# GLA outputs transposed in 32x32 blocks on VectorE and placed by the DRAM round trip, with the head scale in the gating

## The chip, the cores and the metric

The kernel runs on one core of a Trainium2 chip. The metric is the device time of one execution in microseconds. Three runs of the kernel before gave 1454.77 us in the median (1454.15 to 1455.24). The profile is of one further execution, whose span from the first to the last instruction is 1455.4 us.

## The reference, cut to what matters

One inference layer is computed for a prompt of 1024 tokens and for 8 sample tokens. The normalised input is multiplied with one wide matrix; from the product three branches are made, each gated by a SiLU of its own columns, and merged:

```python
h = rmsnorm(x, norm_gain)
q, k, v, gla_g, a_lr, u, pool_g, xq, xg, merge = jnp.split(h @ w_in, split_pts, axis=-1)
o, S = gla_chunked(q, k, v, log_a, S0)                  # 4 heads, values of 256
o = rmsnorm(o, gla_gain.reshape(GLA_HEADS, GLA_DV))     # per head, with a gain per value column
br_gla = o * jax.nn.silu(gla_g)
p, new_hist = multiscale_pool(u, pool_hist, pos0, pool_w, pool_scale)   # windows 2/4/8/16, then a 256x256 map
br_pool = p * jax.nn.silu(pool_g)
br_x = cross_attn(xq, mem_k, mem_v) * jax.nn.silu(xg)
merged = sum over the branches of sigmoid(merge_n) * (br_n @ w_branch[n])
y = x + merged @ w_out
```

The change touches the path from `o` to `br_gla` for the prompt tokens: the recurrence gives `o` with tokens on the partitions, and the gating wants it with value columns on the partitions.

## The kernel before, in words

**The wide product.** `w_in` is taken in pairs of 128 columns (class `Pair`). A pair is done with seven products instead of eight (a Strassen-like scheme): `operands` (L291-315) makes seven left operands a11, a12, s2, s1, s3, s4, a22 from the loaded weights `raw`, on VectorE the sums `ws` (L302), and of each operand a high and a low part: the high part by a copy on ScalarE (L221, tiles `a11h`, `s4h`, ...) and the low part by a subtraction on VectorE (L222, tiles `a11l`, `s4l`, ...). Parts live in a ring of 8 buffers (`W2`, L127). `product` (L533) does one of the seven products: two halves `c` of 258 columns, 4 x 3 matmuls each (high by high L240, high by low L241, low by high L242). `run_product` (L541) puts the results together: a product's result in PSUM is saved by a ScalarE copy (L550, tiles `r1`, `r2`, `r3`), and VectorE adds products to it (L598 for the second product, L615 for the fifth, L624 for the sixth), which releases the PSUM banks `p.z` and `p.x`, of which six exist (`PX`, L96). The order of products (`seq`, L334) is 0 to 4 of a pair, then product 0 of the next pair, then 5 and 6.

**The gated pairs.** The last twelve pairs carry the gates: `gate` applies SiLU, `finish` (L562) multiplies with the branch's output `mix` (L571), then with the sample columns (L573), and sends the tile to DRAM. `mixed(e)` (L580) loads the branch's output tiles `mix` from `mix_scr` on SyncE (L649, in `loaded`) one product ahead of their use. The gated pairs are, in order, those of cross-attention (n = 2), of the GLA branch (n = 0), and of pooling (n = 1). The GLA ones stand at about 915 to 1007 us.

**What fills the products.** After each half product `emit` (L1231) puts steps of two other streams between the matmuls (`fill`, L1222): first cross-attention and the GLA recurrence (from about 390 to 760 us), then, while the GLA gates are computed, pooling. Pooling goes group by group (`w` = 2, 4, 8, 16) and chunk by chunk of 256 tokens: `windows(c)` makes the trailing sums `sw` by 1 to 4 doublings on VectorE (L1143), the mean minus token `df` (L1151; L1149 and L1150 for the first tokens), and its high and low part (`dfh` on ScalarE, `dfl` on VectorE); `mixed(c)` multiplies `dfh` and `dfl` with the group's map in 12 matmuls into a bank `pz` (L240-242 with `dfh`, `dfl`), of which two exist.

**The GLA outputs.** `gla_out(h, c)` (L964) is called 16 times, for 4 heads and 4 chunks. `on` holds 256 tokens by 256 values, as two blocks of 128 tokens. Four TensorE transposes (L971) bring it into a bank `pz`, two ScalarE copies with the head's gain as scale (L973) bring it to `go`, and a DMA from the GpSimd queue (L974) writes it to `mix_scr`.

**What sets the order.** TensorE and SyncE issue in the order in which the program is written (`manual_schedule`, L94). The instructions of VectorE, ScalarE and GpSimd are put into an order by the framework's scheduler when the kernel is built; the order is then fixed, and each engine goes through its list in order, waiting at an instruction until its inputs are there.

Of the kernel before, what the change touches and what calls it, by code (L numbers as in the profile page):

```python
# [14 lines left out]
AF = mybir.ActivationFunctionType  # L15
ALU = mybir.AluOpType
AX = mybir.AxisListType

P = 128
D = 1024  # L20
T = 1024
# [3 lines left out]
NH = 4  # L25
DK = 128
DV = 256
# [6 lines left out]
CT = 256  # L34
# [13 lines left out]
def trunk_kernel(ctx: ExitStack, tc: tile.TileContext,  # L48
# [3 lines left out]
    nc = tc.nc  # L52
# [21 lines left out]
    def act(out, x, func, **kw):  # L74
        i = nc.scalar.activation(out, x, func, **kw)
        if func in (AF.Sigmoid, AF.Silu):
            table["others"].append(i)
            for e in table["exps"]:
                tc.add_manual_dep(i.ins, e.ins.name, nosync, reason="table set")
        else:  # L80
            tc.add_manual_dep(i.ins, table["load"].ins.name, nosync, reason="table set")
            table["new"].append(i)
        return i
# [12 lines left out]
    def PX():  # L96
        return ps.tile([P, 512], F32, tag="px", name="px", bufs=6)

    def PZ():
        return ps.tile([P, 512], F32, tag="pz", name="pz", bufs=2)  # L100

    def shaped(t, shape):
        n = math.prod(shape)
        t = t[:, :n]
        if len(shape) == 2:
            t = t.rearrange("p (a b) -> p a b", a=shape[0])
        elif len(shape) == 3:
            t = t.rearrange("p (a b c) -> p a b c", a=shape[0], b=shape[1])
        return t

    def E(shape, dt=F32, name="e"):
        return shaped(ep.tile([P, EW], dt, tag="e", name=name), shape)

    def R(shape, dt=F32, name="r"):

        return shaped(wk.tile([P, 512], dt, tag="ring", name=name, bufs=NR), shape)
# [13 lines left out]
    def Q(name):  # L130
        return wk.tile([P, QT], F32, tag="q", name=name, bufs=5)
# [5 lines left out]
    ident = cp.tile([P, P], F32, name="ident")  # L137
# [27 lines left out]
    ngain, ggain, pscale, bav = vec[:, 0:8], vec[:, 8:16], vec[:, 16:24], vec[:, 24:28]  # L165
# [35 lines left out]
    def scratch(n, name, shape):  # L201
        return [dr.tile(list(shape), F32, name=f"{name}{i}") for i in range(n)]
# [5 lines left out]
    al_scr = scratch(2, "als", (P, HT))  # L208
    q_scr, k_scr, v_scr4 = (scratch(n, s, PAIR) for n, s in ((2, "qsc"), (2, "ksc"), (4, "vsc")))
    u_scr, xq_raw = (scratch(4, s, PAIR) for s in ("usc", "xqsc"))  # L210
    mix_scr = [scratch(4, f"mixsc{n}_", (P, 2, T)) for n in range(3)]
    m_scr = [scratch(4, f"msc{n}_", PAIR) for n in range(3)]
    br_scr = [scratch(4, f"brsc{n}_", PAIR) for n in range(3)]

# [318 lines left out]
    def product(acc, n, start):  # L533
        i, j = seq[n]
        lh, ll = left[i, j]
        for c in range(2):
            for k in range(4):
                hi, lo = ops[RIGHT[j]][k // 2]
                rh, rl = (x[:, k % 2, c * QT:(c + 1) * QT] for x in (hi, lo))
                mm3(acc[c][:, :QT], lh[:, k, :], ll[:, k, :], rh, rl, start and k == 0, k == 3, not start)  # L540
            yield c  # L541

    def run_product(n):

        i, j = seq[n]
        p = pairs[i]

        def saved(acc, c, name):
            r = Q(name)
            nc.scalar.activation(r, acc[c][:, :QT], AF.Copy)  # L550
            return r

        def piece(t, h, c):
            return t[:, h, c * QT:(c + 1) * QT]

        def diagonal(x, e):

            if e == 0:
                return x[:, 0:16].rearrange("p (a b) -> p a b", b=4)[:, 0:4:3]
            return x[:, 4:12].rearrange("p (a b) -> p a b", b=4)  # L560

        def finish(t, e):  # L562
            rows = (slice(0, 4, 3), slice(1, 3))[e]
            if p.s0 is not None:
                nc.gpsimd.tensor_copy(diagonal(smp[:, NS * p.s0:], e), t[:, :, 512:HT])
            if p.gated:
                n, g = p.gated
                for i in range(2):
                    ch, hf = divmod((0, 3, 1, 2)[2 * e + i], 2)
                    m = p.mix[e][i]  # L570
                    nc.vector.tensor_tensor(t[:, i, :512], t[:, i, :512], m, op=ALU.mult)  # L571
                ss = diagonal(brs[n].rearrange("p k b -> p (k b)")[:, 2 * NS * g:], e)
                nc.vector.tensor_tensor(t[:, :, 512:HT], t[:, :, 512:HT], ss, op=ALU.mult)  # L573
            nc.gpsimd.dma_start(out=p.dst[:, rows, :], in_=t)

        def gate(t, h):
            if p.gated:
                act(t[:, h], t[:, h], AF.Silu)

        def mixed(e):  # L580

            if p.gated:
                n, g = p.gated
                for i in range(2):
                    ch, hf = divmod((0, 3, 1, 2)[2 * e + i], 2)
                    p.mix[e].append(loaded(mix_scr[n][g][:, ch, 512 * hf:512 * hf + 512], [512], "mix"))

        if j == 0:
            p.x = [PX() for _ in range(2)]
            p.r1, p.mix = [], ([], [])  # L590
            for c in product(p.x, n, True):
                p.r1.append(saved(p.x, c, "r1"))
                yield
        elif j == 1:
            y = [PX() for _ in range(2)]
            p.e1 = E([2, HT], name="c1")
            for c in product(y, n, True):
                nc.vector.tensor_tensor(piece(p.e1, 0, c), y[c][:, :QT], p.r1[c], op=ALU.add)  # L598
                if c:
                    gate(p.e1, 0)  # L600
                yield
        elif j == 2:
            p.r2 = []
            for c in product(p.x, n, False):
                p.r2.append(saved(p.x, c, "r2"))
                yield
        elif j == 3:
            p.z = [PX() for _ in range(2)]
            mixed(0)
            for c in product(p.z, n, True):  # L610
                yield
        elif j == 4:
            for c in product(p.x, n, False):
                r3 = saved(p.x, c, "r3")
                nc.vector.tensor_tensor(piece(p.e1, 1, c), p.z[c][:, :QT], r3, op=ALU.add)  # L615
                if c:
                    gate(p.e1, 1)
                    finish(p.e1, 0)
                yield
        elif j == 5:  # L620
            p.e2 = E([2, HT], name="c2")
            mixed(1)
            for c in product(p.z, n, False):
                nc.vector.tensor_tensor(piece(p.e2, 0, c), p.z[c][:, :QT], p.r2[c], op=ALU.add)  # L624
                if c:
                    gate(p.e2, 0)
                yield
        else:
            for c in product(p.x, n, False):
                dst = piece(p.e2, 1, c)  # L630
                if p.gated:
                    act(dst, p.x[c][:, :QT], AF.Silu)
                else:
                    nc.scalar.activation(dst, p.x[c][:, :QT], AF.Copy)
                if c:
                    finish(p.e2, 1)
                yield
# [6 lines left out]
    def mix_chunk(n, h, c):  # L644
        return mix_scr[n][h][:, :, c * CT:(c + 1) * CT]

    def loaded(src, shape, name, alloc=None):
        t = (alloc or R)(shape, name=name)
        nc.sync.dma_start(out=t, in_=src)  # L649
        return t  # L650
# [313 lines left out]

    def gla_out(h, c):
        on, _ = gla["o", h, c]
        g = R([2, CT], name="go")
        t = PZ()
        for i in range(2):
            for j in range(2):  # L970
                nc.tensor.transpose(t[:, i * CT + j * P:i * CT + (j + 1) * P], on[:, j, i * P:(i + 1) * P], ident)  # L971
        for i in range(2):
            nc.scalar.activation(g[:, i], t[:, i * CT:(i + 1) * CT], AF.Copy, scale=ggain[:, 2 * h + i:2 * h + i + 1])  # L973
        nc.gpsimd.dma_start(out=mix_chunk(0, h, c), in_=g)  # L974

    def gla_rows(h):

# [308 lines left out]
    with tc.issue_after(last["hi"].ins), tc.issue_after(last["lo"].ins):  # L1286
        prepare(1)
        for j in (4, 6):
            r = squares(x_t[j:j + 2], 4 + j)
# [166 lines left out]
    for hf, order in enumerate(ORDERS):  # L1456
        for tb in order:
            m = P if tb < 8 else NS
# [22 lines left out]
            n, a = hf, 0  # L1481
            for b in ends:
                t = ts if tb == 8 else begun.pop(0) if begun else PX()
# [13 lines left out]
                n, a = n + 1, b  # L1497
# [3 lines left out]
            if end:  # L1501
                r = rstd_of(sq[:, 2:3], 1.0 / D, more=so_far)
# [6 lines left out]
            r = rstd_of(sq[:, 0:1], 1.0 / D, m)  # L1509
# [34 lines left out]
```

## Time and profile before

| what | before |
|---|---|
| median of 3 runs | 1454.77 us |
| span of the profiled execution | 1455.4 us |
| TensorE matmuls busy | 1430.4 us, 98 % |
| TensorE weight loads busy | 1369.2 us, 94 % |
| VectorE busy | 896.6 us, 62 % |
| ScalarE busy | 688.4 us, 47 % |
| GpSimd busy | 159.0 us, 11 % |
| mean granted TensorE clock | 0.998 |
| DMA traffic | 259.46 MB, 181843 packets |

The page names engines PE, PEld (weight loads of TensorE), DVE (VectorE), ACT (ScalarE), POOL (GpSimd) and SP (SyncE). A group's row reads: line, engine, operation, out<-in tile names, count, then durations. A row of the timeline gives the start and the duration in microseconds; an instruction's successor on the same engine can start before the duration is over, so steps are read as differences of starts. A "q" behind an engine's name is its sequencer, which issues DMAs and waits. The matmul ends are modelled, so that a busy TensorE is not one at its peak.

### The profile page before, as it was taken

What the parts mean: (1) busy time and instruction counts of PE and PEld (TensorE: products, weight loads), DVE (VectorE), ACT (ScalarE), POOL (GpSimd) and SP (SyncE); (2) the same over time, 40 slices, a digit from 0 to 9 for tenths busy, and PEclk for the clock granted to TensorE, in tenths of its full rate; (3) what the DMA queues carried; (4) which work ended last, traced back from release to release, by engine and by line L of the source; (5) the groups of instructions that cost most, each with busy time, mean ns of one, the idle gap of its engine ahead of it and who ended that gap; (6) DMA issues with size and microseconds to landing.
All of it is one profiled execution on the core that took longest, in us unless ns stands there. A gap on an engine that the chain in (4) does not pass through costs nothing.

```text
span 1455.4 us, 28240 instructions
## 1 busy us (share of the span) xinstructions
PE 1430.4 (98%) x10817; PEld 1369.2 (94%) x10817; DVE 896.6 (62%) x2075; ACT 688.4 (47%) x1591; POOL 159.0 (11%) x297
## 2 busy tenths in 40 slices
PE   7999999999999999999999999999999999999998
PEld 6899999999899999999999999999999999999876
DVE  6955756656576767766756668785672443544436
ACT  5744444444565666656554445454472333233312
POOL 3211111111011111111111111110010000000000
PEclk9999999999999999999999999999999999999999
DMA  9345675756445453553544455464595677632633
GB/s 322 127 165 183 204 226 173 227 174 201 158 146 178 149 176 121 166 175 118 180 139 141 153 187 187 147 197 155 191 304 159 219 252 249 231 120 67 230 119 116
DMA packets 181843, 259.46 MB, mean 178 GB/s; under 512 B 20540, under 2 KB 130900, under 8 KB 181700
## 3 DMA queue, kind: packets, MB, share of 16 engines
q1 hardware_dynamic: 159900, 183.87, 40.8%
q0 software_dynamic: 21664, 73.59, 13.3%
q8 instruction: 85, 1.39, 0.4%
q14 instruction: 50, 0.41, 0.1%
q10 hardware_dynamic: 144, 0.20, 0.0%
HBM read 180.47 MB, written 77.59 MB: 177 GB/s over the span
## 4 chain that ended last, share of the span: by engine, by line
PE 87%; DMA 6%; DVE 4%; ACT 1%; issue 1%; SPq 0%; DVEq 0%; POOL 0%; ACTq 0%
PE px L240 25%; PE px L241 24%; PE px L242 24%; PE pz L242 2%; PE pz L240 2%; PE pz L241 2%; DMA qb<-xqs 2%; DMA raw<-in_w_in_dram 1%; DMA vc<-in_cache_mem_v_dram 1%; DVE kc L756 1%; PE pz L942 1%; PE pz L924 1%; DMA wm<-in_w_mv_dram 1%; PE pz L796 1%; PE pz L926 1%
## 5 line engine op out<-in xcount | busy, mean ns | idle before, releaser
L242 PE MATMUL px<-bh,wbl 128*128 128x384 f32 (+1 forms) x576 | 184.1, 320 | 0.0
L241 PE MATMUL px<-bl,wbh 128*128 128x384 f32 (+1 forms) x576 | 184.1, 320 | 0.0
L240 PE MATMUL px<-bh,wbh 128*128 128x384 f32 (+1 forms) x576 | 183.8, 319 | 0.0
L550 ACT ACTIVATE r<-px 128x258 f32<-128x258 f32 x240 | 89.8, 376 | 46.7 <-PE px L242 46.1
L240 PEld LDWEIGHTS px<-bh,wbh 128*128 128x128 f32 x576 | 108.4, 188 | 0.0
L241 PEld LDWEIGHTS px<-bl,wbh 128*128 128x128 f32 x576 | 108.2, 188 | 0.0
L242 PEld LDWEIGHTS px<-bh,wbl 128*128 128x128 f32 x576 | 108.2, 188 | 0.0
L240 PE MATMUL px<-ot,s1h 128*128 128x258 f32 x320 | 93.9, 293 | 0.0
L240 PE MATMUL px<-ot,s3h 128*128 128x258 f32 x320 | 93.4, 292 | 0.0
L240 PE MATMUL px<-o,a12h 128*128 128x258 f32 x320 | 93.3, 291 | 0.0
L240 PE MATMUL px<-o,s4h 128*128 128x258 f32 x320 | 93.0, 291 | 0.2 <-DVE c L615 0.2
L240 PE MATMUL px<-o,a11h 128*128 128x258 f32 x320 | 92.9, 290 | 0.0
L240 PE MATMUL px<-ot,a22h 128*128 128x258 f32 x320 | 92.9, 290 | 0.0
L240 PE MATMUL px<-ot,s2h 128*128 128x258 f32 x320 | 92.3, 288 | 0.0
L241 PE MATMUL px<-o,a11h 128*128 128x258 f32 x320 | 91.0, 284 | 0.3 <-DVE o L222 0.3
L242 PE MATMUL px<-o,a12l 128*128 128x258 f32 x320 | 90.7, 283 | 0.0
L241 PE MATMUL px<-o,a12h 128*128 128x258 f32 x320 | 90.6, 283 | 0.0
L241 PE MATMUL px<-ot,s2h 128*128 128x258 f32 x320 | 90.1, 282 | 0.5 <-DVE ot L222 0.5
L242 PE MATMUL px<-o,a11l 128*128 128x258 f32 x320 | 90.6, 283 | 0.0
L241 PE MATMUL px<-ot,a22h 128*128 128x258 f32 x320 | 90.5, 283 | 0.0
L242 PE MATMUL px<-ot,s3l 128*128 128x258 f32 x320 | 90.4, 283 | 0.0
L241 PE MATMUL px<-ot,s3h 128*128 128x258 f32 x320 | 90.4, 282 | 0.0
(469 smaller groups left out, 4587.3 us busy)
## 6 DMA issues: line engine op xcount, KB each, us to landing
raw<-in_w_in_dram SPq DMA_DIRECT2D x80, 512.0 KB, 3.8
msc<-c POOLq DMA_DIRECT2D x24, 516.0 KB, 4.4
brsc<-c POOLq DMA_DIRECT2D x24, 516.0 KB, 4.0
sig<-msc SPq DMA_DIRECT2D x24, 516.0 KB, 6.0
mix<-mixsc SPq DMA_DIRECT2D x48, 256.0 KB, 4.5
brr<-brsc SPq DMA_DIRECT2D x48, 256.0 KB, 5.3
wbr<-in_w_branch_dram SPq DMA_DIRECT2D x24, 512.0 KB, 5.5
acc<-sig POOLq DMA_DIRECT2D x16, 516.0 KB, 6.1
```

Of the source, the lines that this page charges most:

```text
L240: nc.tensor.matmul(out, lhsT=lh, rhs=rh, start=start, stop=False, skip_group_check=more)
L241: nc.tensor.matmul(out, lhsT=lh, rhs=rl, start=False, stop=False, skip_group_check=more)
L242: nc.tensor.matmul(out, lhsT=ll, rhs=rh, start=False, stop=stop, skip_group_check=more)
L550: nc.scalar.activation(r, acc[c][:, :QT], AF.Copy)
L756: nc.vector.tensor_tensor_reduce(kc[:, a, :], kc[:, a, :], qb[:, bb, :], scale=1.0, scalar=0.0, op0=ALU.mult, op1=ALU.add, accum_out=sc[:, ...
L796: nc.tensor.matmul(t[32 * j:32 * j + 32, :DV], lhsT=pm[:, a, 4 * i + j, :], rhs=vc[j][:, a, :], start=a == 0, stop=a == 1)
L924: nc.tensor.matmul(t[0:64, 0:P], lhsT=ki[:, 0:64], rhs=qi, start=True, stop=True)
L926: nc.tensor.transpose(t[:, P:2 * P], kt, ident)
L942: nc.tensor.matmul(to, lhsT=kiqi[:, 1, cs], rhs=st, start=False, stop=True)
```

## The change

`gla_out` no longer uses TensorE or ScalarE. One VectorE instruction transposes `on` (128 x 512) inside each 32x32 block, and the tile goes to a new DRAM scratch `on_scr[h]`. That has a row of 1 KB for each block of 32 tokens and each value column modulo 32; in a row the eight blocks of columns follow each other, with 32 tokens each. `mixed(e)`, for n = 0 alone, then loads each 128x512 tile `mix` by four DMAs of 32 partitions each, which gather 16 pieces of 32 numbers (128 bytes) per partition; a call issues eight such DMAs where it issued two, in 8 calls. `finish`, for n = 0 alone, multiplies with the gain and with `mix` in one SCALAR_TENSOR_TENSOR instead of the TENSOR_TENSOR.

```diff
-    mix_scr = [scratch(4, f"mixsc{n}_", (P, 2, T)) for n in range(3)]
+    mix_scr = [None if n == 0 else scratch(4, f"mixsc{n}_", (P, 2, T)) for n in range(3)]
+    on_scr = scratch(NH, "onsc", (T // 32, 32, DV))
...
-                    nc.vector.tensor_tensor(t[:, i, :512], t[:, i, :512], m, op=ALU.mult)
+                    if n == 0:
+                        nc.vector.scalar_tensor_tensor(t[:, i, :512], m, ggain[:, 2 * g + ch:2 * g + ch + 1],
+                                                       t[:, i, :512], op0=ALU.mult, op1=ALU.mult)
+                    else:
+                        nc.vector.tensor_tensor(t[:, i, :512], t[:, i, :512], m, op=ALU.mult)
...
-                    p.mix[e].append(loaded(mix_scr[n][g][:, ch, 512 * hf:512 * hf + 512], [512], "mix"))
+                    if n == 0:
+                        m = R([512], name="mix")
+                        for b in range(4):
+                            c0 = ch * P + 32 * b
+                            nc.sync.dma_start(out=m[32 * b:32 * b + 32].rearrange("r (t c) -> r t c", c=32),
+                                              in_=on_scr[g][16 * hf:16 * hf + 16, :, c0:c0 + 32]
+                                              .rearrange("t r c -> r t c"))
+                        p.mix[e].append(m)
+                    else:
+                        p.mix[e].append(loaded(mix_scr[n][g][:, ch, 512 * hf:512 * hf + 512], [512], "mix"))
...
     def gla_out(h, c):
         on, _ = gla["o", h, c]
-        g = R([2, CT], name="go")
-        t = PZ()
-        for i in range(2):
-            for j in range(2):
-                nc.tensor.transpose(t[:, i * CT + j * P:i * CT + (j + 1) * P], on[:, j, i * P:(i + 1) * P], ident)
-        for i in range(2):
-            nc.scalar.activation(g[:, i], t[:, i * CT:(i + 1) * CT], AF.Copy, scale=ggain[:, 2 * h + i:2 * h + i + 1])
-        nc.gpsimd.dma_start(out=mix_chunk(0, h, c), in_=g)
+        g = R([2, DV], name="go")
+        nc.vector.transpose(g.rearrange("p j v -> p (j v)"), on.rearrange("p j v -> p (j v)"))
+        nc.gpsimd.dma_start(out=on_scr[h][8 * c:8 * c + 8].rearrange("(j q) r v -> (q r) j v", j=2), in_=g)
```

Lines of the changed kernel are named by its own numbers in the rows below: L223 there is L222 before, L222 is L221, L303 is L302, L551 is L550, L612, L629 and L638 are L598, L615 and L624, L1152 is L1143, L1158 to L1160 are L1149 to L1151, and L573 is the new SCALAR_TENSOR_TENSOR.

TensorE's order is the same but for the 64 transposes that are gone. The orders of VectorE and ScalarE change in the stretch of the GLA gates, at 915 to 1007 us of the kernel before. Two places follow.

**First place: VectorE before the pooling matmuls of the last group (`w` = 16), first chunk.** Before, the window sums and `df`, and after them `dfl_12807`, stand ahead of `a11l_12944`, the low part of the next pair's first operand:

```order
L1143 TENSOR_TENSOR sw_12800<-sw_12798 128x257
L573 TENSOR_TENSOR c2_12839<-c2_12839,brs0_120 128x2x4
L1149 TENSOR_TENSOR f_12802<-sw_12800,rc_93 128x16
L1151 SCALAR_TENSOR_TENSOR df_12781<-sw_12800,u_12774 128x240
L1150 TENSOR_TENSOR df_12781<-f_12802,u_12774 128x16
L222 TENSOR_TENSOR s3l_12908<-ws_12905,s3h_12907 128x512
L598 TENSOR_TENSOR c1_12915<-px_12913,r1_12769 128x258
L222 TENSOR_TENSOR dfl_12807<-df_12781,dfh_12806 128x512
L1143 TENSOR_TENSOR sw_12962<-u_12777 128x271
L598 TENSOR_TENSOR c1_12915<-px_12914,r1_12829 128x258
L222 TENSOR_TENSOR a11l_12944<-raw_12714,a11h_12943 128x512
```

In the changed kernel `a11l_12860` comes first, then the last sum of the first half (`sw_12698`) and one L612; behind these three stand the twelve rows up to the same low part, now `dfl_12717`:

```order
L1158 TENSOR_TENSOR f_12700<-sw_12698,rc_93 128x16
L1160 SCALAR_TENSOR_TENSOR df_12691<-sw_12698,u_12681 128x240
L1159 TENSOR_TENSOR df_12691<-f_12700,u_12681 128x16
L1152 TENSOR_TENSOR sw_12704<-u_12684 128x271
L612 TENSOR_TENSOR c1_12831<-px_12830,r1_12739 128x258
L1152 TENSOR_TENSOR sw_12706<-sw_12704 128x269
L1152 TENSOR_TENSOR sw_12708<-sw_12706 128x265
L1152 TENSOR_TENSOR sw_12710<-sw_12708 128x257
L1158 TENSOR_TENSOR f_12712<-sw_12710,rc_93 128x16
L1160 SCALAR_TENSOR_TENSOR df_12691<-sw_12710,u_12684 128x240
L1159 TENSOR_TENSOR df_12691<-f_12712,u_12684 128x16
L223 TENSOR_TENSOR dfl_12717<-df_12691,dfh_12716 128x512
```

So thirteen instructions now stand between `a11l` and `dfl`, where `dfl` stood three rows ahead of `a11l`.

**Second place: ScalarE and VectorE around the third chunk of the same group.** `r3` is the copy of half 0 of the fifth product (s3). On ScalarE before, `dfh_13190` stands eight rows ahead of `r3_13372`, and a11h, s4h and a22h of the next operands stand ahead of it too:

```order
L221 ACTIVATE dfh_13190<-df_13171 128x512
L221 ACTIVATE a11h_13287<-raw_13060 128x512
L75 ACTIVATE c1_13259<-c1_13259 128x516
L1164 ACTIVATE po_13198<-pz_13199,vec_90 128x256 x2
L550 ACTIVATE r2_13303<-px_13101 128x258
L221 ACTIVATE s4h_13320<-ws_13133 128x512
L550 ACTIVATE r2_13317<-px_13102 128x258
L221 ACTIVATE a22h_13354<-raw_12911 128x512
L550 ACTIVATE r3_13372<-px_13101 128x258
```

In the changed kernel `r3_13306` stands ahead of all four:

```order
L551 ACTIVATE r2_13245<-px_13024 128x258
L551 ACTIVATE r3_13306<-px_13023 128x258
L222 ACTIVATE a11h_13215<-raw_12982 128x512
L222 ACTIVATE s4h_13248<-ws_13055 128x512
L222 ACTIVATE a22h_13288<-raw_12827 128x512
L75 ACTIVATE c1_13187<-c1_13187 128x516
L222 ACTIVATE dfh_13118<-df_13099 128x512
```

On VectorE the rows a11l, s4l, a22l, L612 twice and then `L629 c1_13187<-px_13252,r3_13306` stand there in this order, and behind them the whole of the third chunk's windows:

```order
L1152 TENSOR_TENSOR sw_13100<-u_12900 128x271
L1152 TENSOR_TENSOR sw_13102<-sw_13100 128x269
L1152 TENSOR_TENSOR sw_13104<-sw_13102 128x265
L1152 TENSOR_TENSOR sw_13106<-sw_13104 128x257
L573 SCALAR_TENSOR_TENSOR c2_13061<-mix_13062,vec_90,c2_13061 128x512
L1160 SCALAR_TENSOR_TENSOR df_13099<-sw_13106,u_12900 128x256
L1152 TENSOR_TENSOR sw_13109<-u_12903 128x271
L1152 TENSOR_TENSOR sw_13111<-sw_13109 128x269
L1152 TENSOR_TENSOR sw_13113<-sw_13111 128x265
L1152 TENSOR_TENSOR sw_13115<-sw_13113 128x257
L1160 SCALAR_TENSOR_TENSOR df_13099<-sw_13115,u_12903 128x256
L223 TENSOR_TENSOR dfl_13119<-df_13099,dfh_13118 128x512
```

Before, `dfl_13191` stands eleven rows ahead of the L615 that reads `r3_13372`. On TensorE, before and now, the twelve pooling matmuls of this chunk stand between half 0 and half 1 of the s3 product.

The same turn of `r3_13895` ahead of a11h, s4h and a22h, and of a11l, s4l and a22l ahead of the two L612, stands once more at the end of the last GLA gate pair (36th pair of the program), without a pooling chunk.

## Prediction

> **What bounds the kernel now.** I read the page's head first, then the chain that ended last, then the timeline of single engines at 940 to 975 us.
>
> ```profile
> span 1455.4 us, 28240 instructions
> PE 1430.4 (98%) x10817; PEld 1369.2 (94%) x10817; DVE 896.6 (62%) x2075; ACT 688.4 (47%) x1591; POOL 159.0 (11%) x297
> ```
>
> TensorE is the bound: 98 % of the span is matmuls. So two things count alone: TensorE instructions that go, and new places where TensorE waits. The span stands 0.6 us above the median of 1454.77 us; I sum changes against the span and take them off the median. About 0.2 % (2.9 us) is what a measurement of this kernel can tell from no change.
>
> The chain, at one of the 16 removed sets (start, length, what), and at the one set where TensorE waited:
>
> ```profile
> 513.12 0.44 PE pz L971 x4
> 513.55 0.12 PE px L240
> ...
> 755.21 0.50 ACT on L960
> ```
>
> The set stands in an unbroken row of matmuls, each 0.12 us long. Nothing covers it.
>
> The stretch of the GLA gates, where the new loads and the new order lie (columns: stretch, its length, busy time and count of PE, PEld, DVE, ACT, POOL, granted clock, DMA share, GB/s):
>
> ```profile
> 915.00:1007.00 92.00, 92.00 (x773) 91.90 (x772) 67.50 (x148) 43.18 (x92) 10.38 (x18) 1.00 0.52 167
> ```
>
> TensorE has no gap there, VectorE is busy for 73 % of it. TensorE's freedom from gaps hangs on VectorE being ahead of it at each hand-over.
>
> **The change part by part.**
>
> *TensorE transposes out.* 16 sets of 0.44 us on the chain are 7.0 us. Of the 0.50 us wait for `on` at the last set I take 0.4 as gained, between nothing (the next step may wait for the same ScalarE work) and all of it. Together -7.4 us, from -7.0 to -7.5.
>
> *ScalarE copies out.* 32 copies of L973 leave an engine that is busy 47 %; nothing on the chain waits for them. Zero.
>
> *VectorE transposes in.* 16 instructions on 128x512, which the trace does not show. The nearest rows are the other 128x512 operations of VectorE at 0.68 us (below); twice that, 1.4 us, is my upper end, zero the lower since an added instruction cannot give time. VectorE is idle for 38 % of the span, and by the order they stand right behind the state update, a place where TensorE has matmuls of the wide product to go on with. 16 x 0.68 = 11 us of VectorE work, hidden; if the cover were gone at each head's end, four times 0.7. I take 0.
>
> *The gain in `finish`.* A SCALAR_TENSOR_TENSOR for a TENSOR_TENSOR of the same size: zero; were it twice the 0.68 us, 16 x 0.7 us would come at VectorE's idle 27 %.
>
> *The loads of `mix`.* Now 64 DMAs of 512 pieces of 128 bytes where 16 of 128 pieces of 2 KB stood.
>
> ```profile
> L649 SPq DMA_DIRECT2D mix<-mixsc x16: 319/406/1321, 915.7 to 996.1; - x16
> ```
>
> ```profile
> 946.85 1.23 SPq L649 DMA_DIRECT2D mix<-mixsc  x2
> ```
>
> ```profile
> q1 hardware_dynamic: 159900, 183.87, 40.8%
> ```
>
> These are the group of the issues (shortest, median and longest in ns), one call in SyncE's timeline, and the page's row of the queue (packets, MB, share of 16 engines over the span).
>
> SyncE needs 0.41 us per issue (the median), so eight take 3.3 us instead of 0.8; calls come some 10 us apart, and raw weights queued behind them come 2.5 us later. A packet of this queue took 0.408 x 16 x 1455.4 / 159900 = 59 ns for 1150 bytes on the mean. By bytes, a call's 4096 pieces need 0.5 MB x 59 ns / 1150 / 16 = 1.7 us of all engines; at a full mean packet each, 15 us. I take 5 us, nearer to the bytes: the first tile is complete 1.6 + 5 = 6.6 us after its first issue, the second 8.3. The call at 946.85 is used at 954.33 (row below), 7.5 us later, the second tile later still. Hidden; the bad end is a rival.
>
> *The order of VectorE and ScalarE.* This part decides. The rows of the kernel before (start, length):
>
> ```profile
> 939.53 0.17 DVE L1149 TENSOR_TENSOR f<-sw,rc 128x16 f32<-128x16 f32 x1
> 939.63 0.40 DVE L1151 SCALAR_TENSOR_TENSOR df<-sw,u 128x240 f32<-128x240 f32 x1
> 939.95 0.17 DVE L1150 TENSOR_TENSOR df<-f,u 128x16 f32<-128x16 f32 x1
> ...
> 940.97 0.68 DVE L222 TENSOR_TENSOR dfl<-df,dfh 128x512 fp32r<-128x512 f32 x1
> ...
> 942.38 0.69 DVE L222 TENSOR_TENSOR a11l<-raw,a11h 128x512 fp32r<-128x512 f32 x1
> 942.99 0.43 DVE L1143 TENSOR_TENSOR sw<-sw 128x269 f32<-128x269 f32 x1
> 943.34 0.68 DVE L571 TENSOR_TENSOR c<-c,mix 128x512 f32<-128x512 f32 x1
> ...
> 954.33 0.68 DVE L571 TENSOR_TENSOR c<-c,mix 128x512 f32<-128x512 f32 x1
> ...
> 965.38 0.69 DVE L222 TENSOR_TENSOR dfl<-df,dfh 128x512 fp32r<-128x512 f32 x1
> ```
>
> From start to start a 128x512 step takes 0.60, a `sw` or an add of 258 columns 0.35, `df` 0.32, the two 16-column steps 0.1 each. On ScalarE:
>
> ```profile
> 941.72 0.63 ACT L221 ACTIVATE a11h<-raw 128x512 fp32r<-128x512 f32 x1 [0.94 <-PE px L241]
> ...
> 946.04 0.63 ACT L221 ACTIVATE s4h<-ws 128x512 fp32r<-128x512 f32 x1 [2.42 <-PE px L241]
> 946.58 0.37 ACT L550 ACTIVATE r<-px 128x258 f32<-128x258 f32 x1
> ...
> 971.98 0.39 ACT L550 ACTIVATE r<-px 128x258 f32<-128x258 f32 x1 [0.86 <-PE px L242]
> ```
>
> And TensorE, where the pooling matmuls start:
>
> ```profile
> 943.03 0.28 PE L240 MATMUL pz<-dfh,pwh 128*128 128x256 f32 x1
> ...
> 971.66 0.28 PE L242 MATMUL px<-ot,s3l 128*128 128x258 f32 x1
> 971.78 0.28 PE L240 MATMUL pz<-dfh,pwh 128*128 128x256 f32 x1
> ...
> 973.22 0.28 PE L240 MATMUL px<-ot,s3h 128*128 128x258 f32 x1
> ```
>
> First place. `dfl` was ready at 941.65 (940.97 + 0.68), 1.4 us before TensorE came. a11l cannot start ahead of 942.38: its high part on ScalarE was released by TensorE at 941.72. In the new order `df` follows it: a11l 0.60, five sums 1.75, two adds 0.70, f and df twice 0.84, and the last one's end 0.1 make 4.0; then `dfh` 0.63 and `dfl` 0.68. So `dfl` is there at 942.4 + 5.3 = 947.7 instead of 941.65, and TensorE, due at 943.03, waits 4.7 us (4.2 to 5.7, a tenth of the chain either way). VectorE and ScalarE go on meanwhile, but all that TensorE needs next stands behind.
>
> Second place. `dfl` was ready at 966.07 (965.38 + 0.69) for matmuls due at 971.78. Now ScalarE must do r3 first, which needs the s3 half that ends just ahead of those matmuls (971.66 + 0.28; r3 started at 971.98). Then: r3 0.37, a11h, s4h, a22h 3 x 0.54 and the last one's end 0.1, a22l 0.60, two L612 0.70, L629 0.35, four sums 1.40, the gate's multiplication 0.60, df 0.34, four sums 1.40, df 0.42, dfh 0.63, dfl 0.68: 9.2 us after 971.98, that is 981.2, a wait of 9.3. If a11l, s4l, a22l and the two L612 were done earlier, 2.9 less: 6.4 is the lower end; 10 the upper.
>
> Third place, the end of the 36th pair: half 1 of s3 covers 1.44 us (971.78 to 973.22 is another 12 matmuls); r3 to a22l takes 2.7 as above, and the first L612, which frees the bank for the next pair's first product, 0.4 more: 1.9 us of waiting (0 to 2.5).
>
> The other chunks of this group keep 3 us (second) and about nothing (fourth) in hand; I add 0, at most 1.
>
> *What such a wait does to the clock.* The trace shows it once (columns as in the stretch above, the granted clock behind POOL):
>
> ```profile
> 123.00:124.00 1.00, 0.32 (x2) 0.30 (x2) 0.92 (x3) 0.63 (x2) 0.83 (x2) 1.00 1.05 358
> 124.00:125.00 1.00, 0.71 (x4) 0.53 (x3) 0.42 (x1) 0.00 (x0) 0.12 (x1) 0.77 1.29 287
> 125.00:126.00 1.00, 1.00 (x7) 1.00 (x6) 0.00 (x0) 0.00 (x0) 0.00 (x0) 0.50 0.58 83
> 126.00:127.00 1.00, 1.00 (x7) 1.00 (x7) 0.01 (x1) 0.00 (x0) 0.00 (x0) 0.50 0.80 209
> 127.00:128.00 1.00, 1.00 (x6) 1.00 (x6) 0.68 (x1) 0.29 (x1) 0.00 (x0) 0.53 1.06 370
> ```
>
> After a stretch with two or three matmuls per us the granted clock falls to 0.50. The missing shares are 0.23 + 0.50 + 0.50 + 0.47 = 1.7 us of full-speed time lost. Both long waits are emptier, so 2 x 1.7 = 3.4 us (0 if the clock holds, 5.1 if the longer one stays slow twice as long). The Trainium skill, "TensorE: Matmul & The Clock Gate", Part 1, states that an idle window of about 3.4 us halves the clock until a busy window has passed. The trace agrees: 1.7 us lost at half speed is 3.4 us. It speaks against the change.
>
> *Sum.* -7.4 + 4.7 + 9.3 + 1.9 + 3.4 = +11.9 us. The ends: -7.5 + 4.2 + 6.4 + 0 + 0 = +3.1, and -7.0 + 5.7 + 10 + 2.5 + 1 + 5.1 = +17.3.
>
> **The rivals.**
>
> *Faster: the waits are covered.* If VectorE ran far enough ahead, or TensorE had other matmuls to do, only the transposes' 7.4 us would show: 1447.4 us. For it: before, TensorE never stood still in this stretch, and VectorE is idle for 27 % of it. Against: both engines go in order, r3 cannot precede its own product, and the pooling matmuls are next on TensorE. It decides if `df` comes ahead of a11l and r3 on the chip. Chance 0.11.
>
> *The waits are short.* If they come to 7 us with no clock loss, the two sides balance: about 1455 to 1458. Chance 0.10.
>
> *The waits come, the clock holds.* The windows may be judged over longer stretches than the one above. 11.9 - 3.4 = 8.5: 1463.3. Chance 0.22.
>
> *Late loads.* At 15 us per call plus 3.3 of issue, `mix` comes some 5 us late in each of 8 calls: 40 us more, about 1506. For it: 4096 packets where 256 were. Against: the queue is busy 41 % of the span, and a mean packet that is nine times as long takes 59 ns. The Trainium skill, "DMA: Bandwidth & Descriptors", Rules for kernel authors, warns that a transpose by a plain DMA with a rearranged pattern is 19 times slower; no row here shows it. By that figure, an estimate, the 1.7 us by bytes would become 32 us a call, and the eight calls would add some 200 us. Chance 0.07.
>
> **How the numbers follow.** The likeliest case, waits with a clock loss, has 0.50: 1454.77 + 11.9 = 1466.7 us. The range starts at 1455, with the balanced case, and ends at 1454.77 + 17.3 = 1472; what it leaves out is the faster case and the late loads, 0.18. Faster by over 0.2 %: 0.12, the covered waits and a little of the balanced case. Within 0.2 %: 0.05. Slower: 0.83.
>
> **What would show it.** In the profile after: no L971 rows, span 7 us shorter up to 915 us; then idle time of PE ahead of the pooling matmuls with `dfh` and `dfl`, 4 to 5 us near 936 and 8 to 10 us near 970, put down to VectorE's `dfl` or ScalarE's `dfh`, and a granted clock of 0.5 for some 3 us behind each. VectorE idle on DMA `mix` for more than a few us would show late loads instead. The forecast is wrong if PE is still busy throughout 915 to 1007.

## The result, and the profile after

The changed kernel took 1474.8 us in the median of 4 runs (1473.9 to 1476.2), the kernel before, run beside it, 1454.5 us (1452.9 to 1455.2). The ratio is 1.0138, with a 95 % interval of 1.0126 to 1.0151: slower by 20 us. The forecast was 1466.7 us, with 1472 as the upper end. The direction was right, and so were the places that the forecast named. The size was not.

The head of the page after:

```profile
span 1472.5 us, 28140 instructions
PE 1428.1 (97%) x10753; PEld 1364.6 (93%) x10753; DVE 906.9 (62%) x2091; ACT 676.0 (46%) x1559; POOL 159.3 (11%) x297
```

TensorE has 64 instructions less and a longer span: it now waits. The list of its waits (what waited, for whom: us in total, times, longest) says for whom; these are the rows that the kernel before does not have in this size:

```profile
PE pz L241 <- ACT dfh L222: 13.9, 2, 9.6
...
PE px L241 <- ACT c L75: 2.8, 2, 2.1
PE pz L938 <- DVE akvl L223: 2.6, 1, 2.6
PE px L241 <- DVE c L612: 1.9, 1, 1.9
...
PE pz L242 <- DVE dfl L223: 0.7, 2, 0.3
```

The table by stretches, after (stretch, length, busy time and count of PE, PEld, DVE, ACT, POOL, granted clock, DMA share, GB/s). The first row is the stretch that had 92.00 of 92.00 us of TensorE before:

```profile
915.00:1007.00 92.00, 76.53 (x607) 75.11 (x606) 54.29 (x118) 32.14 (x68) 6.87 (x13) 0.93 0.50 121
915.00:1040.00 125.00, 105.53 (x844) 103.69 (x843) 72.94 (x154) 45.17 (x97) 9.94 (x18) 0.95 0.51 131
```

```profile
936.00:940.00 4.00, 0.00 (x0) 0.00 (x0) 3.31 (x13) 1.46 (x3) 0.00 (x0) 1.00 0.43 68
940.00:944.00 4.00, 3.52 (x15) 3.33 (x16) 0.69 (x1) 0.08 (x1) 0.00 (x0) 0.59 0.84 183
944.00:950.00 6.00, 6.00 (x52) 6.00 (x51) 3.94 (x9) 1.87 (x4) 0.00 (x0) 0.99 0.03 10
...
972.00:981.00 9.00, 0.15 (x2) 0.00 (x0) 7.62 (x17) 2.57 (x5) 0.00 (x0) 0.66 0.14 36
981.00:985.00 4.00, 3.10 (x13) 2.81 (x14) 1.35 (x2) 1.36 (x3) 1.24 (x2) 0.50 1.12 243
```

TensorE stands still for 4 us at 936 and for 9 us at 972, while VectorE is busy for 3.3 of the 4 and 7.6 of the 9 us: it is doing the window sums that the order put in front of `dfl`. Behind the standstills the granted clock is 0.59 and 0.50 over one stretch of 4 us each. The timeline of TensorE at the first place (start, length, what, idle time before it and who ended it):

```profile
935.52 0.28 PE L243 MATMUL px<-ot,s2l 128*128 128x258 f32 x1
940.13 0.38 PE L241 MATMUL pz<-dfh,pwh 128*128 128x256 f32 x1 [4.33 <-ACT dfh L222]
940.86 0.58 PE L242 MATMUL pz<-dfl,pwh 128*128 128x256 f32 x1 [0.34 <-DVE dfl L223]
941.24 0.42 PE L243 MATMUL pz<-dfh,pwl 128*128 128x256 f32 x1
941.46 0.42 PE L241 MATMUL pz<-dfh,pwh 128*128 128x256 f32 x1
```

VectorE's at the same place shows what it did instead, from the `a11l` that now comes first to the `dfl` that TensorE waits for:

```profile
934.99 0.69 DVE L223 TENSOR_TENSOR a11l<-raw,a11h 128x512 fp32r<-128x512 f32 x1 [0.86 <-ACT a11h L222]
...
939.25 0.17 DVE L1159 TENSOR_TENSOR df<-f,u 128x16 f32<-128x16 f32 x1
...
940.11 0.69 DVE L223 TENSOR_TENSOR dfl<-df,dfh 128x512 fp32r<-128x512 f32 x1 [0.69 <-ACT dfh L222]
```

From `a11l` to the end of `dfl` are 5.8 us; the forecast had 5.3. ScalarE at the second place, `r3` and the `dfh` that stands behind it:

```profile
972.18 0.39 ACT L551 ACTIVATE r<-px 128x258 f32<-128x258 f32 x1 [3.92 <-PE px L243]
...
981.07 0.63 ACT L222 ACTIVATE dfh<-df 128x512 fp32r<-128x512 f32 x1 [4.72 <-DVE df L1160]
```

To see where the 20 us arose, I matched the TensorE instructions of both traces one by one (the transposes left out) and took start after minus start before. At 374 us, ahead of the first removed set, the difference is -3.4: the start-up differs from execution to execution (in the traces of the other runs this difference is -0.8 to -4.9), and says nothing of the change. From there to the end it goes to +17.1, that is +20.5, close to the 20.3 of the medians. All figures of this table come from one execution of each kernel. By places:

| where | forecast | measured |
|---|---|---|
| 16 sets of transposes, and the wait for `on` | -7.4 | -8.2 |
| waits of the recurrence near 640 us, clock behind them | 0 | +4.2 |
| first place, wait | +4.7 | +5.1 |
| clock behind it | +1.7 | +1.5 |
| two waits at the a12 product (`c`, L75) | 0 | +3.2 |
| second place, wait | +9.3 | +10.4 |
| clock behind it | +1.7 | +1.2 |
| fourth chunk, `dfl` | 0 | +0.7 |
| third place, wait | +1.9 | +2.3 |
| sum | +11.9 | +20.4 |

The three places with their clock cost 20.5 us where 19.3 were forecast. What is missing are places that the forecast did not list or took at nothing: 8.1 us.

### The profile page after: what moved, and what is told of

Its sections match the earlier page's. It is cut to its first block, busy times and chain, and to the rows that moved or that the text cites. A ratio compares the mean times of both kernels' runs of the same rounds, so it can differ in the third digit from the quotient of the medians.

```text
span 1472.5 us, 28140 instructions
## 1 busy us (share of the span) xinstructions
PE 1428.1 (97%) x10753; PEld 1364.6 (93%) x10753; DVE 906.9 (62%) x2091; ACT 676.0 (46%) x1559; POOL 159.3 (11%) x297
## 4 chain that ended last, share of the span: by engine, by line
PE 83%; DMA 5%; DVE 5%; issue 5%; ACT 1%; SPq 0%; POOL 0%; DVEq 0%; ACTq 0%; POOLq 0%
PE px L241 24%; PE px L242 23%; PE px L243 23%; PE pz L243 2%; PE pz L242 2%; DMA qb<-xqs 2%; PE pz L241 2%; DMA raw<-in_w_in_dram 1%; DMA vc<-in_cache_mem_v_dram 1%; DVE kc L770 1%; PE pz L956 1%; PE pz L938 1%; DMA x<-in_x_prompt_dram 1%; PE pz L810 1%; PE pz L940 1%
## 5 line engine op out<-in xcount | busy, mean ns | idle before, releaser
L551 ACT ACTIVATE r<-px 128x258 f32<-128x258 f32 x240 | 89.6, 376 | 64.9 <-PE px L243 63.0
L241 PE MATMUL px<-o,a12h 128*128 128x258 f32 x320 | 93.0, 291 | 2.8 <-ACT c L75 2.8
L243 PE MATMUL px<-ot,s2l 128*128 128x258 f32 x320 | 90.6, 283 | 0.0
```

Of the source, the lines that this page charges most:

```text
L241: nc.tensor.matmul(out, lhsT=lh, rhs=rh, start=start, stop=False, skip_group_check=more)
L243: nc.tensor.matmul(out, lhsT=ll, rhs=rh, start=False, stop=stop, skip_group_check=more)
```

## The experiments

**The theories.** *Order*: the 64 small loads are not late themselves; that they stand in the program, in this form, makes the scheduler build another order of VectorE and ScalarE, and the waits come from that. *Transfer*: the loads in 128-byte pieces, or their issue on SyncE, are late or slow something on the chip. *VectorE work*: the 16 transposes take VectorE time where it is short. All ratios are against the kernel before, with 95 % intervals. The edits are against the changed kernel, where nothing else is said.

**Loads in one piece, placing left out (x1).**

```diff
-                        for b in range(4):
-                            c0 = ch * P + 32 * b
-                            nc.sync.dma_start(out=m[32 * b:32 * b + 32].rearrange("r (t c) -> r t c", c=32), ...)
+                        flat = on_scr[g].rearrange("t r v -> (t r) v").rearrange("(p a) v -> p (a v)", p=P)
+                        c0 = 1024 * ch + 512 * hf
+                        nc.sync.dma_start(out=m, in_=flat[:, c0:c0 + 512])
```

> The changed kernel, but each mix tile of the GLA gates is loaded by one DMA with 2 KB pieces instead of four with 128-byte pieces (the numbers land in the wrong places, so this leaves out the placing). VectorE transposes and the gain in the gating stay. Both the order theory (the waits come from where the scheduler puts VectorE's and ScalarE's work) and the late-load theory (the 128-byte loads are slow on the chip) expect no long wait at 915 to 1030 us and 1447 to 1451 us. The theory that the VectorE transposes cost the time expects 1470 us or more.

1447.7 us, ratio 0.9954 (0.9938 to 0.9969). The gates' stretch has no wait:

```profile
915.00:1040.00 125.00, 125.00 (x1047) 124.96 (x1046) 90.02 (x189) 56.44 (x118) 11.60 (x18) 1.00 0.52 165
```

So the waits among the gates hang on the loads; the VectorE transposes and the gain in `finish` are in this kernel too and bring none there. Whether it is the time of the loads or the order that they bring, this run alone does not say.

**TensorE transposes back, small loads kept (x2).** The values reach the gating in other places than the reference has them, and the gain is applied twice.

```diff
-        nc.vector.transpose(g.rearrange("p j v -> p (j v)"), on.rearrange("p j v -> p (j v)"))
+        (the four TensorE transposes and two ScalarE copies of the kernel before)
```

> The changed kernel with the TensorE transposes and ScalarE copies of before in gla_out in place of the VectorE transpose; the 128-byte loads stay (the layout in DRAM is then not the one that the loads assume, so the placing is wrong). Order theory: the two orders in the stretch of the GLA gates are those of the changed kernel, so all its waits return and the transposes' 7 us come on top, while the wait near 644 us in the GLA stretch goes: 1476 to 1481 us. Late loads: the same 1476 to 1481. VectorE transposes as the cause: 1455 us or less.

1477.7 us, ratio 1.0163 (1.0139 to 1.0187). The main wait is the same to the tenth, without one VectorE transpose in the kernel:

```profile
PE pz L241 <- ACT dfh L222: 13.9, 2, 9.6
```

VectorE's transposes have no part in this wait.

**The same 64 loads into another pool of buffers (x3).** One word: the tile comes from a pool of four 2 KB buffers instead of the ring of 14.

```diff
-                        m = R([512], name="mix")
+                        m = V([512], name="mix")
```

> The changed kernel with one word changed: the mix tiles of the GLA gates come from the pool of four buffers that the sample states used, not from the ring of fourteen. Loads, pieces, queues and instructions are the same; the scheduler makes another order, in which the pooling windows stand ahead of the operands again in most places. Order theory: 1450 to 1456 us, the two long waits shrink to under 3 us together and the clock stays up behind them. Late loads, or VectorE transposes: 1470 us or more, since both are untouched.

1452.5 us (10 runs), ratio 0.9983 (0.9967 to 0.9999). It has the same 64 loads, and an issue takes as long as in the changed kernel (there 303/487/2152 ns; shortest, median, longest, then from, to):

```profile
L595 SPq DMA_DIRECT2D mix<-onsc x64: 302/487/2206, 905.7 to 996.8; - x64
```

The waits for `dfh` are gone:

```profile
PE px L241 <- DVE c L612: 2.6, 2, 1.9
...
PE pz L938 <- DVE akvl L223: 1.9, 1, 1.9
...
PE px L241 <- ACT c L75: 1.4, 2, 1.0
```

```profile
915.00:1040.00 125.00, 120.59 (x999) 119.57 (x999) 85.30 (x181) 53.68 (x115) 11.00 (x17) 1.00 0.58 158
```

This tells order from transfer: the chip moves the same pieces from the same places by the same queue, and 22 us go. Besides the built order, the word changes for which buffer a load waits: in the changed kernel SyncE had two waits, of 14.0 and 9.3 us, put down to a late `df`, before it could issue a load, and here it has four of 5.7 us together. That did not reach TensorE by way of a late load. In the changed kernel's trace the waits of VectorE and ScalarE between 905 and 1036 us name each other, TensorE and the landing of `brsc` stores, and no load (three waits of 2.0 us and less name nothing; the kernel before has such too); ahead of the multiplications by `mix` VectorE sat idle for 0.2 us in all, for ScalarE.

What stays in x3 is 0.7 us at the third place, a wait of the same kind of 1.9 us one pair earlier (both are in the L612 row), and 1.4 us at the a12 product.

**Order held by hints as well (x4).** On top of x3, the a11 parts may not be issued ahead of the last pooling `dfh` and `dfl`, and `r3` with its add not ahead of the a22 parts. The lines that keep these instructions in `held` and `tail` are left out here.

```diff
+                    if name == "a11" and "lo" in held:
+                        order.enter_context(tc.issue_after(held["hi"].ins))
+                        order.enter_context(tc.issue_after(held["lo"].ins))
...
+                    if p.gated and p.gated[0] == 0 and hasattr(p, "tail"):
+                        order.enter_context(tc.issue_after(p.tail[0].ins))
+                        order.enter_context(tc.issue_after(p.tail[1].ins))
```

> As the run with the mix tiles in the other pool, and three order hints besides (no waits): the operands a11 of the next pair are queued behind the last pooling low part, and r3 and its add behind a22's parts. Order theory: the wait at the end of the 36th pair goes too, 1447 to 1453 us. Late loads, or VectorE transposes: 1470 us or more.

1452.8 us (10 runs), ratio 0.9990 (0.9972 to 1.0008). No gain over x3 in the median. The expectation that the wait at the end of the 36th pair goes did not come true: 0.7 us stay there as in x3, the wait of the pair before goes from 1.9 to 1.5, and 1.0 us stays at the a12 product:

```profile
PE px L241 <- DVE c L618: 2.2, 2, 1.5
...
PE px L241 <- ACT c L75: 1.0, 1, 1.0
```

Against the trace of before, this one is 11.1 us ahead at 756 us and 6.0 at the end: 5 us are given back in the gates' stretch, where x3 gave back 5.8 (from 10.0 to 4.2). The long waits that the hints were written against had gone with x3 already.

**Placing at the store, loads as before (x5).** GpSimd's store writes each 32-token, 128-column piece into the old layout, 16 DMAs per call; the loads of `mix` are again one DMA of 2 KB pieces each.

```diff
-        nc.gpsimd.dma_start(out=on_scr[h][8 * c:8 * c + 8].rearrange("(j q) r v -> (q r) j v", j=2), in_=g)
+        for q in range(4):
+            for ch in range(2):
+                for j in range(2):
+                    t0 = c * CT + j * P + 32 * q
+                    nc.gpsimd.dma_start(out=mix_scr[0][h][:, ch, t0:t0 + 32].rearrange("(b r) t -> r b t", r=32),
+                                        in_=g[32 * q:32 * q + 32, j, ch * P:ch * P + P].rearrange("r (b t) -> r b t", t=32))
```

> The placing is moved from the load to the store: after the VectorE transpose, 16 DMAs per call on the GpSimd queue write the 32x32 blocks to their place in the old scratch in pieces of 128 bytes, and the mix tiles are loaded in 2 KB pieces as before. The same result as the reference's. Order theory: VectorE's and ScalarE's order in the stretch of the GLA gates is that of before, no long wait, 1446 to 1451 us. If small pieces themselves cost time on this chip, their 256 stores would show: the stores of the wide product's results queue behind them on GpSimd, and the time would be 1455 us or more.

1447.1 us, ratio 0.9946 (0.9931 to 0.9960): faster than both kernels. It does all that the change wanted, with no wait among the gates:

```profile
span 1445.6 us, 28375 instructions
PE 1420.4 (98%) x10753; PEld 1359.8 (94%) x10753; DVE 907.1 (63%) x2091; ACT 677.0 (47%) x1559; POOL 286.4 (20%) x537
```

```profile
915.00:1040.00 125.00, 125.00 (x1046) 124.96 (x1045) 89.65 (x189) 56.43 (x118) 11.67 (x20) 1.00 0.51 165
```

GpSimd is busy 127 us longer with the 256 issues, and no wait of TensorE is put down to it or to its stores; VectorE has one of 2.5 us, near 633 us, put down to the landing of a `go` store. VectorE's work in sum is that of the changed kernel (907 us both). In the recurrence TensorE has two waits for VectorE; the first is at the product that the last experiments are about, and whether the transposes cause them is not shown:

```profile
PE pz L928 <- DVE akvl L222: 1.6, 1, 1.6
...
PE pz L240 <- DVE akvl L222: 1.0, 1, 1.0
```

**Only the order, in the kernel before (x8).** Transposes and loads untouched; the window sums of the last pooling group are written later in the program, right ahead of their use.

```diff
-                if c < 3:
+                if c < 3 and g < 3:
                     windows(c + 1)
...
+                if c and g == 3:
+                    windows(c)
                 mixed(c)
```

> The kernel before with its TensorE transposes and 2 KB loads; only in the last pooling group the windows of a chunk are written down right ahead of its matmuls instead of one chunk earlier, so that the scheduler puts them later. Order theory: at least one pooling chunk finds its low part missing by about 6 us, and the clock falls behind that wait for 1.5 us more: 1459 to 1464 us. If the order does not matter, 1454 to 1455 us.

1463.6 us, ratio 1.0065 (1.0049 to 1.0082): slower by 9 us without any part of the change, with a wait of the changed kernel's kind, here at the second chunk, and the clock loss behind it:

```profile
PE pz L240 <- ACT dfh L221: 5.2, 1, 5.2
```

```profile
915.00:1040.00 125.00, 119.60 (x983) 119.00 (x982) 82.86 (x175) 54.97 (x116) 11.63 (x20) 0.97 0.46 151
```

A late `df` alone is enough. The matched traces give +7.4 us between 374 us and the end: 4.9 for the wait, 2.5 for `dfl` and the slow matmuls behind it.

**The wait near 640 us (x6, x7, x9, x10).** It belongs to the recurrence: the first product with `kiqi` (L938) waits for VectorE. The kernel before waited 0.5 us at this product:

```profile
PE pz L924 <- DVE akvl L222: 0.5, 1, 0.5
```

The changed kernel, TensorE's timeline there:

```profile
640.69 0.28 PE L243 MATMUL px<-o,a12l 128*128 128x258 f32 x1
643.56 0.29 PE L938 MATMUL pz<-kiqi 128*64 128x128 f32 x1 [2.59 <-DVE akvl L223]
...
644.58 0.56 PE L241 MATMUL px<-ot,s2h 128*128 128x258 f32 x1
...
645.37 0.42 PE L241 MATMUL px<-ot,s2h 128*128 128x258 f32 x1
645.59 0.42 PE L242 MATMUL px<-ot,s2h 128*128 128x258 f32 x1
```

The matmuls behind it stand 0.22 us apart instead of 0.12, and the granted clock is 0.50 from 644 to 647 us: half clock once more. Four kernels on top of x4 ask whether VectorE's transposes cause the wait: two transposes per call instead of one (x6), none, with `on` stored as it is (x7), a ScalarE copy in their place (x9), and none before the store but two whose results nobody reads (x10). The diff shows the lines of all four together; `g2` is a second tile like `g`.

```diff
-        nc.vector.transpose(g.rearrange("p j v -> p (j v)"), on.rearrange("p j v -> p (j v)"))
+        nc.vector.transpose(g2.rearrange("p j v -> p (j v)"), on.rearrange("p j v -> p (j v)"))   # x6, x10
+        nc.vector.transpose(g.rearrange("p j v -> p (j v)"), g2.rearrange("p j v -> p (j v)"))    # x6, x10
+        nc.scalar.activation(g, on, AF.Copy)                                                      # x9
-        nc.gpsimd.dma_start(out=on_scr[h]..., in_=g)
+        nc.gpsimd.dma_start(out=on_scr[h]..., in_=on)                                             # x7, x10
```

> The run with the order kept, and in gla_out two VectorE transposes one after the other instead of one (the second turns the first back, so the placing is wrong). Order theory, transposes hidden: no difference to the run with the order kept beyond 2 us, 1450 to 1455 us. If VectorE in the GLA stretch is at its limit and the wait near 640 us comes from the transposes: up to 16 x 0.7 = 11 us more, with a wait near 640 us of 3 us or more.

> The run with the order kept, without any transpose: the GLA outputs are written as they are (the placing is wrong; it leaves out the 16 VectorE transposes). Order theory, transposes hidden: 1449 to 1454 us, within 2 us of the run with the order kept. If the transposes cause the wait near 640 us: 1446 to 1449 us and no wait there.

> The run with the order kept, with a plain ScalarE copy in place of the VectorE transpose in gla_out (the placing is wrong; no transposes). The store keeps its time after a copy, VectorE has nothing extra. If the wait near 640 us comes from VectorE's extra work: none there and 1447 to 1450 us, as without transposes. If it comes from the store of the copied tile that falls between the loads of the sample states: a wait of 0.5 to 2.7 us there as with the transposes, 1450 to 1454 us.

> The run without transposes, with two VectorE transposes per call whose result nobody reads; the store takes the untransposed tile at once (the placing is wrong). If the wait near 640 us comes from VectorE's extra work: a wait of 2 us or more there and 1450 to 1454 us. If it comes from the store's time: no wait there, 1447 to 1450 us.

| kernel | us | ratio (95 %) | wait at the first `kiqi` product |
|---|---|---|---|
| x4, one transpose | 1452.8 | 0.9990 (0.9972 to 1.0008) | 0.3 |
| x6, two | 1452.3 | 0.9979 (0.9962 to 0.9997) | 2.6 |
| x7, none | 1448.7 | 0.9960 (0.9945 to 0.9975) | none |
| x9, ScalarE copy | 1452.2 | 0.9987 (0.9973 to 1.0001) | none |
| x10, two unread | 1450.3 | 0.9975 (0.9961 to 0.9989) | none |

```profile
PE pz L948 <- DVE akvl L223: 2.6, 1, 2.6
```

This is x6's row. In these single executions the longer waits stand where VectorE makes the tile that is stored (x1, x3, x5, x6 and the changed kernel: 1.2 to 2.6 us); x2, x7, x9 and x10 have none. But x4 is such a kernel too, and its row is this:

```profile
PE pz L948 <- DVE akvl L223: 0.3, 1, 0.3
```

The changed kernel, x3 and x4 go through the same instructions of VectorE, ScalarE and GpSimd in the same order from 382 to 755 us, and their waits are 2.6, 1.9 and 0.3. So the length of this wait differs by over 2 us between executions of the same work, and one trace of each kernel cannot tell what causes it. What the three have in common is the distance from one VectorE step on the sample states `s`; the rows are of the changed kernel, x3 and x4:

```profile
635.14 0.48 DVE L1019 SCALAR_TENSOR_TENSOR s<-vb,smp,s 128x256 f32<-128x256 f32 x1 [3.69 <-PE pz L942]
```

```profile
633.89 0.48 DVE L1019 SCALAR_TENSOR_TENSOR s<-vb,smp,s 128x256 f32<-128x256 f32 x1 [2.44 <-ACT s L1018]
```

```profile
632.97 0.49 DVE L1029 SCALAR_TENSOR_TENSOR s<-vb,smp,s 128x256 f32<-128x256 f32 x1 [1.47 <-ACT s2h L222]
```

The product follows 8.4 us behind each of them (at 643.56, 642.31 and 641.39), so the later this step starts, the longer TensorE waits. What holds it is put down to another engine in each of the three, and to loads of `vb` in x2, x7 and x9; what it is stays open.

The four runs do not decide between their theories either. x6 was within 2 us of x4, as expected for hidden transposes, so that doubling the work cost nothing in the median. x7 met the other expectation, no wait and 1446 to 1449 us. x9 met neither: no wait, but the time that was expected with one. x10 had no wait with twice the work, and its 1450.3 lies where its two ranges meet. The intervals of all four overlap that of x4.

## Why the prediction was right in direction and wrong in size

**The transposes and the wait for `on`:** -7.4 forecast, -8.2 measured. The sets gave about 0.44 us each, as forecast, but the last one gave 1.8: the list of TensorE's waits before has 0.9 us for `on`, where the forecast read the 0.50 of the chain:

```profile
PE pz L971 <- ACT on L960: 0.9, 1, 0.9
```

x1 and x5 show the same from the other side: with the long waits gone the kernel takes 1447.7 and 1447.1, the 1447.4 of the rival "the waits are covered". That rival was the right account of what the change is worth, in an order without the waits, which the changed kernel does not have.

**The loads:** hidden, as forecast. A DMA of 64 KB in 128-byte pieces landed 4.1 us after its issue in the median:

```profile
mix<-onsc SPq DMA_DIRECT2D x64, 64.0 KB, 4.1
```

and VectorE never sat idle for it ahead of the multiplication. The estimate by the Trainium skill's factor of 19 ("DMA: Bandwidth & Descriptors", Rules for kernel authors) does not hold for these pieces; x3 with the same loads takes 1452.5 us. The page sets this factor against the hardware DMA transpose, which no run here uses.

**The gain and the transposes on VectorE** were priced by the nearest 128x512 rows at 0.68 us each. After (shortest, median, longest in ns; from, to):

```profile
L573 DVE SCALAR_TENSOR_TENSOR c<-mix,vec,c x16: 742/745/751, 924.5 to 1035.9; 128x512 f32<-128x512 f32 x16
L982 DVE STREAM_TRANSPOSE go<-on x16: 700/704/717, 416.4 to 750.1; 128x512 f32<-128x512 f32 x16
```

The prices hold. What the sum had at 0 is the recurrence, where the transposes stand: near 640 us TensorE lost 4.2 us in this pair of traces, of which 0.6 at a product ahead of the `kiqi` product, 2.1 to 2.2 at that product and 1.5 to the clock. The forecast's bound, four times 0.7 if the cover were gone, looked at the added work at each head's end. The wait came once, and x10 had none with twice the work; whether the transposes caused it stays open.

**The order of VectorE and ScalarE:** the deciding step, and its mechanism is shown: x3 and x5 take the order away and the long waits go, x2 keeps it without the VectorE transposes, and x8 makes one such wait in the kernel before, with its loads and transposes. The three named places cost 5.1, 10.4 and 2.3 for 4.7, 9.3 and 1.9. The step that failed is the list of waits: beyond the three places the sum had 0, with at most 1 us for "the other chunks", and 8.1 us were measured there. They are the 4.2 near 640 us, whose cause is open, 3.2 at two a12 products, and 0.7 at the fourth chunk. The a12 waits were not on the list because the forecast did not follow what a late gate does to the buffer of its tile. ScalarE's next `c` waits for the store of an earlier one. The row of the same pair in the kernel before comes first, where ScalarE came right behind TensorE, then the changed kernel's:

```profile
1003.83 0.39 ACT L75 ACTIVATE c<-px 128x258 f32<-128x258 f32 x1 [0.35 <-PE px L242]
```

```profile
1019.42 0.66 ACT L75 ACTIVATE c<-px 128x258 f32<-128x258 f32 x2 [2.09 <-DMA brsc<-c]
```

In the changed kernel a gated tile was done at 1014.3, its store to `brsc` left at 1014.64 and landed at 1019.34, and ScalarE went on at 1019.42. In the new order the tile was finished later, the store left later, and TensorE's a12 product, which needs the bank that this copy empties, lost 0.9 and 2.3 us. I read this from the trace; no run took it out by itself.

**The clock:** 3.4 forecast at two places, 2.7 measured. The Trainium skill, "TensorE: Matmul & The Clock Gate", Part 1, speaks of an idle window of some 3.4 us. The traces agree after the waits of 4.3, 5.2 and 9.6 us. Near 640 us the clock fell too, after an idle time of 2.6 us with seven short matmuls behind it, which is shorter than the window; there the measurement goes further than the rule. A third loss of 1.5 us came from that. By the rival that the clock holds, the forecast would have been 3.4 us further off.

**The sum:** 11.9 forecast; +8.1 from places not listed or taken at nothing (4.2, 3.2, 0.7), +0.4 from the listed ones together (-0.8 at the transposes, +1.2 at the three places), 20.4. That is also above the upper end of the range, 17.3, which had 1 us for other places.

## What to carry to other kernels

Where a framework's scheduler fixes the order of some engines, a changed transfer is first a changed order: read the built order on every engine that feeds the bound one, and follow each late step on to the buffers that it frees, not only to the next consumer. If a rearranged transfer must be paid somewhere, try it on the store side of an idle queue, and try another buffer pool: here the one word in x3 was worth 22 us and the store in x5 another 5. When the matmuls that go are known and unhidden, what is left of their gain is a matter of the new waits alone. In these traces each wait of 2.6 us and more, near 640 us and among the gates, cost a further 1.2 to 1.9 us of half clock behind it. And compare executions of the same kernel before a wait is put down to an edit: the one near 640 us was 2.6, 1.9 and 0.3 us long in three traces of the same order.

## What the runs showed of the hardware

- Loads of 64 KB in 512 pieces of 128 bytes landed in 4.1 us in the median in the changed kernel; the loads of `mix` of 256 KB in 2 KB pieces took 4.5 us before. By bytes that is worse; no engine's wait between 905 and 1036 us was put down to them.
- 256 stores of 16 KB in 128-byte pieces from the GpSimd queue (x5) cost 127 us of that engine; the kernel took 1447.1 us, against 1447.7 for x1, which has the same transposes without these stores.
- One idle time of 2.6 us of TensorE was followed by 2.5 us of matmuls at 0.22 us instead of 0.12 (changed kernel, near 640 us; x6 shows the same after 2.6 us there); idle times of 2.1 us and less in the gates' stretch of the changed kernel were not.
